# The head of a one-layer encoder block: tile 0 scaled ahead of the first low part, norm_g's row spread by two fp32r products, low parts reordered, roots taken from the sum

## The chip, the cores and the metric

The kernel runs on one core of a Trainium2 chip, as one launch. The metric is the device time of one execution in microseconds, the median over several runs. A profile of one execution gives each engine's instructions with start and duration: PE (matrix products; PEld loads its weights), DVE (VectorE), ACT (ScalarE), POOL (GpSimd) and SP, whose queue issues most transfers.

## What is computed

One layer of a gated hybrid block on x of 1024 x 1024 (float32), then a last norm:

```python
def rmsnorm(x, g):
    y = x * lax.rsqrt(jnp.mean(x * x, axis=-1, keepdims=True) + EPS)
    return y * g

h = rmsnorm(x, norm_g)
q, k, v, za, u, vs, zs, gm = jnp.split(h @ w_in, IN_SPLITS, axis=-1)
a = window_sink_attention(rope(q), rope(k), v, sinks)
a = (a * silu(za)) @ w_att_out
sgo = chunked_spatial_gating(gelu(u), gelu(vs), sg_w, sg_b, sg_ln_g, sg_ln_b)
sgo = (sgo * silu(zs)) @ w_sg_out
ga, gs = jnp.split(sigmoid(gm + b_merge), 2, axis=-1)
x = x + (ga * a + gs * sgo) @ w_o
out = rmsnorm(x, final_g)
```

The change concerns three things in it: the first norm of h, the first products of h (with the columns of `vs`), and the reciprocal roots of all norms.

## The kernel before

Products in float32 are made of three products in fp32r, a float32 format that PE reads in one go: each operand is split into a high part (a cast on ACT, `hi`) and a low part (the operand minus its high part, mostly on DVE, `lo`), and high x high, high x low and low x high are summed. Products go by seven instead of eight block products (Strassen-Winograd), which is where the names `b11`, `b21`, `t1`, `b22` and the sums `s1` to `s4` are from.

**The head** brings h into that form, token tile by token tile (128 tokens, `t` from 0 to 7). For a tile, `scale_of` squares the rows on ACT (L545, the sum over a row comes by a read of ACT's accumulator into `ss`), and `rstd_of` (L130) makes the factor 1/root: DVE makes the mean plus EPS (`ve`, L133), ACT its root (L135), DVE the reciprocal (L137), and three small DVE operations one Newton step (L140, L144, L145). `turned_half` scales half of the row by the factor and norm_g (L553, in place), and PE turns it in four 128 x 128 transposes (L557) into a PSUM bank `sc`, of which there are two. `form_of` makes the high part from there on ACT (L568) and the low part on DVE (L569). Tiles 0 to 3 give `b11` and `b21`; tiles 4 to 7 go through `second_tile`, where DVE also subtracts (L595), and ACT copies (L596, L600).

Norm_g is needed on all 128 partitions. Its row lies in one partition (`g_row`); for tiles 0 and 1 PE spreads it by a product of a row of ones with it in float32 (L505) into the two banks `tp` (`g_in`); for the later tiles a transfer brings it (`g_sb`). Products of ones without a use (`keep_busy`, L498) run on PE beside that.

The **first weights** (columns of `vs`) come in four loads, a11 and a12 in two halves each; `split_vs` splits them into high and low parts (L655, L656 for the first half, in two pieces, the second low part on POOL; L155, L156 for the others). `first_product(t)` then makes 24 products of tile t, 12 with a11 into a bank `mm` (or `tp`), 12 with a12 into a bank `o` (all L669), and ACT copies the second away (L687). Later `by_s1` and `by_s4` make the products of tiles 4 to 7 with the sums (L669, ACT's copy L695). Products of the later stages are at L342.

**Order.** Each engine works through its instructions in a fixed order. A scheduler sets that order from the order in which the code issues operations, their dependencies and its own costs; `after(second, first)` binds two instructions of one engine without a wait. Transfers issued on SP run in the order of issue. So code that is written in another order in the head can move instructions of all head tiles on all engines, up to the point where tile 7 is done.

**The tail.** The last product's rows are added to x, squared in two halves on ACT (L1752), the second half's sum goes through `rstd_of` with the first half's mean as `base`, and the row is scaled and stored (L1769 to L1776).

Of the kernel before, what the change touches and what calls it, by code (L numbers as in the profile page):

```python
# [30 lines left out]
P = 128  # L31
# [21 lines left out]
def hybrid_tile(  # L53
# [75 lines left out]

    def rstd_of(ss, scale, base=EPS, n=1):  # L130

        ve = mtile([P, n], F32, f"st{n}", 16 if n == 1 else 5)
        nc.vector.tensor_scalar(ve[:], ss, scale, base, op0=ALU.mult, op1=ALU.add)  # L133
        rt = mtile([P, n], F32, f"st{n}", 16 if n == 1 else 5)
        nc.scalar.activation(rt[:], ve[:], AF.Sqrt)  # L135
# [11 lines left out]

    def split(hi, lo, src, minus=False):
# [5 lines left out]
        else:  # L154
            nc.scalar.copy(hi, src)  # L155
# [339 lines left out]

    def keep_busy(n):
        for _ in range(n):
            nc.tensor.matmul(idle[:], ones_r[:, 0:P], ones_r[:], start=True, stop=True)  # L498

    idle = bank("sc")  # L500
    keep_busy(2)

    g_in = [bank("tp") for half in range(2)]
    for half in range(2):
        nc.tensor.matmul(g_in[half][:], plain[0:1, 0:P], g_row[:, half_of(half)], start=True, stop=True)  # L505
    keep_busy(2)
# [22 lines left out]
    casts, lows, turns = [], [], []  # L529
# [12 lines left out]
    def scale_of(t):  # L542
# [3 lines left out]
        if t == 1 or t > 2:  # L546

            after(square, casts[-1] if t == 1 else casts[2 * t - 3])
        return xt, rstd_of(ss[:], 1.0 / D)

    def turned_half(xt, r, j):
        cs = half_of(j)
        nc.vector.scalar_tensor_tensor(xt[:, cs], xt[:, cs], r[:], g_of[j], op0=ALU.mult, op1=ALU.mult)  # L553
        pt = bank("sc")
        for i in range(4):
            k = j * 4 + i
            turns.append(nc.tensor.transpose(pt[:, i * P : (i + 1) * P], xt[:, k * P : (k + 1) * P], ident[:]))  # L557
        return pt
# [83 lines left out]
    def split_vs(c):  # L642
# [6 lines left out]
        if c:  # L649
            split(hi[:], lo[:], flat(raw))  # L650
        else:

            for k in range(2):
                ks = half_of(k)
                nc.scalar.copy(hi[:, ks], raw[:, k, :])  # L655
                (nc.gpsimd if k else nc.vector).tensor_tensor(  # L656
                    lo[:, ks], raw[:, k, :], hi[:, ks].bitcast(F32), op=ALU.subtract
# [3 lines left out]
    def vs_product(acc, name, t, weight, fresh, last=True, cs=(0, 1)):  # L661
        bh, bl = hb[name]
        for c in cs:
            for n in range(3):
                for k in (2 * c, 2 * c + 1):
# [8 lines left out]
                        stop=k == 3 and n == 2,  # L674
# [7 lines left out]
    def first_product(t):  # L682
        accs[t] = bank("mm" if t < 2 else "tp")
        vs_product(accs[t], "b11", t, "a11", True)
        m2 = bank("o")
        vs_product(m2, "b21", t, "a12", True)
# [38 lines left out]
    for c in (2, 3):  # L725
        split_vs(c)
    for move in unsplit:
# [1184 lines left out]
```

## Time and profile before

| | |
|---|---|
| median of 3 runs | 911.89 us (910.78 to 914.15) |
| the profiled execution | 912.14 us |
| its span, first to last instruction | 910.4 us |
| POOL busy in the span | 141.9 us |
| HBM over the span | 147.74 MB read, 86.11 MB written |

A timeline row reads: start in us, duration, engine, line, operation, output<-input, shapes, count, and in brackets the idle time before it and what ended that. Rows with a count are several instructions; their duration is from the first's start to the last's end. Ends of products on PE are modelled, so two that follow each other overlap in the rows.

### The profile page before, as it was taken

What the parts mean: (1) busy time and instruction counts of PE and PEld (TensorE: products, weight loads), DVE (VectorE), ACT (ScalarE), POOL (GpSimd) and SP (SyncE); (2) the same over time, 40 slices, a digit from 0 to 9 for tenths busy, and PEclk for the clock granted to TensorE, in tenths of its full rate; (3) what the DMA queues carried; (4) which work ended last, traced back from release to release, by engine and by line L of the source; (5) the groups of instructions that cost most, each with busy time, mean ns of one, the idle gap of its engine ahead of it and who ended that gap; (6) DMA issues with size and microseconds to landing.
All of it is one profiled execution on the core that took longest, in us unless ns stands there. A gap on an engine that the chain in (4) does not pass through costs nothing.

```text
span 910.4 us, 13184 instructions
## 1 busy us (share of the span) xinstructions
PE 894.2 (98%) x4284; PEld 743.6 (82%) x4284; DVE 696.8 (77%) x1263; ACT 527.0 (58%) x1059; POOL 141.9 (16%) x204
## 2 busy tenths in 40 slices
PE   8999999999999999999999999999998999999996
PEld 6778888888878788888888888888877887888885
DVE  6869966666676788888878788657797489579986
ACT  7866533334545467767667677654674375367443
POOL 1322222203030001111111011201001111110012
PEclk9999999999999999999999999999999999999999
DMA  9997888858778767788786789899859665998632
GB/s 329 211 250 214 263 204 175 173 153 270 252 235 290 206 181 216 208 178 202 170 239 215 244 224 244 212 345 347 295 192 368 220 197 156 312 307 274 204 120 112
DMA packets 131598, 209.57 MB, mean 230 GB/s; under 512 B 12649, under 2 KB 61033, under 8 KB 131530
## 3 DMA queue, kind: packets, MB, share of 16 engines
q1 hardware_dynamic: 110072, 149.74, 49.7%
q0 software_dynamic: 21312, 58.73, 28.4%
q8 instruction: 34, 0.56, 0.3%
q14 instruction: 34, 0.28, 0.1%
q10 hardware_dynamic: 146, 0.27, 0.1%
HBM read 147.74 MB, written 86.11 MB: 257 GB/s over the span
## 4 chain that ended last, share of the span: by engine, by line
PE 87%; DVE 7%; DMA 2%; issue 1%; ACT 1%; SPq 0%; POOL 0%; DVEq 0%; ACTq 0%
PE ps_mm L342 36%; PE ps_o L342 26%; PE ps_sc L1242 3%; PE ps_tp L342 3%; PE ps_mm L669 3%; PE ps_tp L669 2%; PE ps_o L1327 2%; PE ps_sc L342 2%; PE ps_tp L1286 2%; PE ps_o L669 2%; PE ps_tp L917 2%; PE ps_sc L669 1%; DVE wl L156 1%; DVE bq L185 1%; DMA q_hl<-qhl 1%
## 5 line engine op out<-in xcount | busy, mean ns | idle before, releaser
L155 ACT CAST wh<-s 128x1024 fp32r<-128x1024 f32 (+1 forms) x79 | 79.2, 1005 | 96.0 <-PE ps_mm L342 52.0
L156 DVE TENSOR_TENSOR wl<-wr,wh 128x512 fp32r<-128x512 f32 (+1 forms) x77 | 72.0, 936 | 51.8 <-ACT wh L155 51.0
L156 DVE TENSOR_TENSOR wl<-s,wh 128x1024 fp32r<-128x1024 f32 (+1 forms) x79 | 92.5, 1171 | 12.3 <-ACT wh L155 12.1
L155 ACT CAST wh<-wr 128x512 fp32r<-128x512 f32 (+1 forms) x77 | 63.0, 820 | 58.4 <-PE ps_mm L342 30.4
L342 PE MATMUL ps_o<-T_t1h,wh 128*128 128x512 f32 x148 | 58.8, 397 | 0.8 <-ACT wh L155 0.7
L342 PE MATMUL ps_o<-T_b22h,wh 128*128 128x512 f32 x148 | 58.3, 394 | 0.0
L342 PE MATMUL ps_mm<-T_b11h,wl 128*128 128x512 f32 x140 | 55.4, 396 | 2.9 <-DVE wl L156 2.9
L342 PE MATMUL ps_o<-T_b22l,wh 128*128 128x512 f32 x148 | 57.9, 391 | 0.0
L342 PE MATMUL ps_o<-T_b22h,wl 128*128 128x512 f32 x148 | 57.7, 390 | 0.0
L342 PE MATMUL ps_o<-T_t1h,wl 128*128 128x512 f32 x148 | 57.7, 390 | 0.0
L342 PE MATMUL ps_o<-T_t1l,wh 128*128 128x512 f32 x148 | 57.6, 389 | 0.0
L1255 ACT ACTIVATE pr<-ps_sc,sm 128x192 f32<-128x192 f32 (+2 forms) x128 | 50.9, 410 | 9.0 <-DVE sm L1251 6.6
L342 PE MATMUL ps_mm<-T_b11h,wh 128*128 128x512 f32 x140 | 55.3, 395 | 0.0
L342 PE MATMUL ps_mm<-T_t4h,wh 128*128 128x512 f32 x140 | 55.3, 395 | 0.0
L342 PE MATMUL ps_mm<-T_t2h,wh 128*128 128x512 f32 x140 | 54.7, 391 | 0.6 <-ACT x L360 0.6
L342 PE MATMUL ps_mm<-T_t3l,wh 128*128 128x512 f32 x140 | 54.6, 390 | 0.6 <-DVE T_t3l L156 0.6
L342 PE MATMUL ps_mm<-T_b11l,wh 128*128 128x512 f32 x140 | 55.2, 394 | 0.0
L342 PE MATMUL ps_mm<-T_t3h,wh 128*128 128x512 f32 x140 | 54.9, 392 | 0.0
L342 PE MATMUL ps_mm<-T_t4h,wl 128*128 128x512 f32 x140 | 54.7, 391 | 0.0
L342 PE MATMUL ps_mm<-T_t3h,wl 128*128 128x512 f32 x140 | 54.7, 390 | 0.0
L342 PE MATMUL ps_mm<-T_t2h,wl 128*128 128x512 f32 x140 | 54.6, 390 | 0.0
L342 PE MATMUL ps_mm<-T_t2l,wh 128*128 128x512 f32 x140 | 54.6, 390 | 0.0
(389 smaller groups left out, 2395.2 us busy)
## 6 DMA issues: line engine op xcount, KB each, us to landing
wr<-in_w_dram SPq DMA_DIRECT2D x86, 256.0 KB
sums<-in_w_dram POOLq DMA_DIRECT2D x20, 512.0 KB, 6.7
s<-sums SPq DMA_DIRECT2D x20, 512.0 KB
q_hl<-qhl SPq DMA_DIRECT2D x16, 512.0 KB
q<-q_hl SPq DMA_DIRECT2D x64, 128.0 KB
y_dr<-x POOLq DMA_DIRECT2D x28, 256.0 KB, 6.5
g<-in_w_dram POOLq DMA_DIRECT2D x12, 512.0 KB, 6.0
wr<-in_w_dram SPq DMA_DIRECT2D x11, 512.0 KB
```

Source lines behind the costliest of these rows:

```text
L155: nc.scalar.copy(hi, src)
L156: return nc.vector.tensor_sub(lo, src, hi.bitcast(F32))
L185: op(dst[:, i : i + 2, :], a[:, i : i + 2, :], c[:, i : i + 2, :])
L342: nc.tensor.matmul(acc, lt, rt, start=fresh and k == 0 and n == 0, stop=k == 3 and n == 2, skip_group_check=True,)
L669: mm = nc.tensor.matmul(acc[:], lt, rt, start=fresh and k == 0 and n == 0, stop=k == 3 and n == 2, skip_group_check=True,)
L917: nc.tensor.matmul(pm[:, t * P : (t + 1) * P], xh[:, half * 4 + t, g * P : (g + 1) * P], bias[-1][1][:, g % 4, :], start=True, stop=True,)
L1242: nc.tensor.matmul(sc[:, i, k0:], q_of[:, c, i * P : (i + 1) * P], kt[:, f, k0:], start=f == 0, stop=f == 1,)
L1255: nc.scalar.activation(held_in[c, i], sc[:, i, lo:hi], AF.Exp, bias=nmax[:, c, i : i + 1], scale=-1.0, accum_out=sums[:, c, i : i + 1],)
L1286: nc.tensor.transpose(dst, pr[:, i, block * P : block * P + width], ident[:])
L1327: nc.tensor.matmul(po[:, cs], lt, rt, start=n == 0, stop=n == len(terms) - 1)
```

## The change

Roots are taken from the sum itself (ACT's activation does scale and bias, `of_root`), with the mean made beside it on DVE. Norm_g's row is split into two fp32r parts and spread by four products among eleven from a first string of ten `keep_busy` products, whose order `feed` binds. The second token tile's load is issued before the second weight half, its square stands ahead of tile 0's first cast, and tile 0's scaling stands ahead of the first weight low part. Tile 0's products take their terms in another order.

```diff
     def rstd_of(ss, scale, base=EPS, n=1):
         ve = mtile([P, n], F32, f"st{n}", 16 if n == 1 else 5)
-        nc.vector.tensor_scalar(ve[:], ss, scale, base, op0=ALU.mult, op1=ALU.add)
+        of_mean.append(nc.vector.tensor_scalar(ve[:], ss, scale, base, op0=ALU.mult, op1=ALU.add))
         rt = mtile([P, n], F32, f"st{n}", 16 if n == 1 else 5)
-        nc.scalar.activation(rt[:], ve[:], AF.Sqrt)
+        of_root.append(nc.scalar.activation(rt[:], ss, AF.Sqrt, bias=eps_sb[:] if base is EPS else base, scale=scale))
...
+    def feed(mm):
+        if fed:
+            after(mm, fed[-1])
+        fed.append(mm)
+
     def keep_busy(n):
         for _ in range(n):
-            nc.tensor.matmul(idle[:], ones_r[:, 0:P], ones_r[:], start=True, stop=True)
+            feed(nc.tensor.matmul(idle[:], ones_r[:, 0:P], ones_r[:], start=True, stop=True))
 
     idle = bank("sc")
-    keep_busy(2)
-
     g_in = [bank("tp") for half in range(2)]
+    g_both = slot("t1h")
+    g_parts = [g_both[0:1, 2 * n : 2 * n + 2, :] for n in range(2)]
     for half in range(2):
-        nc.tensor.matmul(g_in[half][:], plain[0:1, 0:P], g_row[:, half_of(half)], start=True, stop=True)
-    keep_busy(2)
+        hi, lo = (part[:, half, :] for part in g_parts)
+        src = g_row[:, half_of(half)]
+        nc.scalar.copy(hi, src)
+        (nc.gpsimd if half else nc.vector).tensor_tensor(lo, src, hi.bitcast(F32), op=ALU.subtract)
+
+    def spread(n, half):
+        part = g_parts[n][:, half, :]
+        feed(
+            nc.tensor.matmul(g_in[half][:], ones_r[0:1, 0:P], part, start=n == 0, stop=n == 1, skip_group_check=True)
+        )
+
+    keep_busy(6)
+    spread(0, 0)
+    spread(0, 1)
+    spread(1, 0)
+    keep_busy(1)
+    spread(1, 1)
+    keep_busy(3)
...
-        if t == 1 or t > 2:
-
-            after(square, casts[-1] if t == 1 else casts[2 * t - 3])
+        squares.append(square)
+        if t > 2:
+
+            after(square, casts[2 * t - 3])
...
         if c:
-            split(hi[:], lo[:], flat(raw))
+            first_lows.append(split(hi[:], lo[:], flat(raw)))
         else:
 
             for k in range(2):
                 ks = half_of(k)
-                nc.scalar.copy(hi[:, ks], raw[:, k, :])
+                after(nc.scalar.copy(hi[:, ks], raw[:, k, :]), of_root[0])
...
-    def vs_product(acc, name, t, weight, fresh, last=True, cs=(0, 1)):
+    def vs_product(acc, name, t, weight, fresh, last=True, cs=(0, 1), terms=(0, 1, 2)):
...
     def first_product(t):
         accs[t] = bank("mm" if t < 2 else "tp")
-        vs_product(accs[t], "b11", t, "a11", True)
+        terms = (0, 1, 2) if t else (0, 2, 1)
+        vs_product(accs[t], "b11", t, "a11", True, terms=terms)
...
-    unsplit = first_tile(0)
+    first = scale_of(0)
     for name, at in (("a11", "t3h"), ("a12", "t3l")):
         raws[name] = slot(at, dt=F32)
     load_vs(0)
+    x_in[1] = load_x(1)
     load_vs(1)
+    first_lows = []
     split_vs(0)
-    x_in[1] = load_x(1)
+    second = scale_of(1)
+    unsplit = first_tile(0, first)
+    after(of_mean[1], lows[0])
+    after(first_lows[0], scalings[1])
+    after(lows[0], first_lows[0])
     split_vs(1)
-    second = scale_of(1)
+    after(first_lows[2], lows[0])
+    after(lows[1], first_lows[2])
+    after(casts[0], squares[1])
+    after(hi_of[0], casts[0])
+    after(casts[1], hi_of[0])
...
     for c in (2, 3):
         split_vs(c)
+        after(first_lows[c + 1], lows[1])
+        after(hi_of[c - 1], casts[1])
...
     first_tile(1, second)
+    after(scalings[2], first_lows[4])
...
-    nc.vector.tensor_scalar(ones[:], ident[:], 0.0, 1.0, op0=ALU.mult, op1=ALU.add)
+    after(nc.vector.tensor_scalar(ones[:], ident[:], 0.0, 1.0, op0=ALU.mult, op1=ALU.add), lows[-1])
```

How this moves the built program's rows, at three places. Line numbers of the changed program are some 20 to 50 higher: L553 is there L582, L569 L601, L568 L600, L545 L572, L656 L689, L156 L160, L155 L159, L695 L730, L596 L628, L557 L587, L669 L703.

DVE in the head, from tile 0's reciprocal to tile 0's second low part (`wr_119` is tile 0 of x, `wl` are weight low parts, `st` the small statistics), before:

```order
L137 RECIPROCAL st_23_147<-st_22_145 128x1
L140 SCALAR_TENSOR_TENSOR st_24_149<-st_21_143,st_23_147 128x1
L144 TENSOR_SCALAR st_24_149<-st_24_149 128x1
L145 TENSOR_TENSOR st_24_149<-st_24_149,st_23_147 128x1
L656 TENSOR_TENSOR wl_174<-T_t3h_169,wh_173 128x512
L553 SCALAR_TENSOR_TENSOR wr_119<-wr_119,st_24_149,ps_tp_126 128x512
L553 SCALAR_TENSOR_TENSOR wr_119<-wr_119,st_24_149,ps_tp_127 128x512
L156 TENSOR_TENSOR wl_182<-T_t3h_169,wh_181 128x1024
L569 TENSOR_TENSOR T_b11l_133<-ps_sc_154,T_b11h_132 128x4x128
L569 TENSOR_TENSOR T_b21l_135<-ps_sc_162,T_b21h_134 128x4x128
L813 TENSOR_SCALAR ones_719<-ident 128x128
```

and now:

```order
L147 TENSOR_TENSOR st_25_162<-st_25_162,st_24_160 128x1
L582 SCALAR_TENSOR_TENSOR wr_119<-wr_119,st_25_162,ps_tp_124 128x512
L582 SCALAR_TENSOR_TENSOR wr_119<-wr_119,st_25_162,ps_tp_125 128x512
L689 TENSOR_TENSOR wl_173<-T_t3h_166,wh_172 128x512
L601 TENSOR_TENSOR T_b11l_146<-ps_sc_191,T_b11h_145 128x4x128
L135 TENSOR_SCALAR st_32_180<-st_31_178 128x1
L160 TENSOR_TENSOR wl_207<-T_t3h_166,wh_206 128x1024
L139 RECIPROCAL st_34_184<-st_33_182 128x1
L601 TENSOR_TENSOR T_b21l_148<-ps_sc_199,T_b21h_147 128x4x128
```

Both scalings stand ahead of the first weight low part, each weight low part has changed places with a token low part, and `ones` is gone from here.

ACT in the head and again at tiles 6 and 7 (`wT` is where the squares go, `ps_sc` a turned half), in the head before:

```order
L135 ACTIVATE st_22_145<-st_21_143 128x1
L655 CAST wh_173<-T_t3h_169 128x512 x2
L155 CAST wh_181<-T_t3h_169 128x1024
L568 CAST T_b11h_132<-ps_sc_154 128x4x128
L568 CAST T_b21h_134<-ps_sc_162 128x4x128
L545 ACTIVATE wT_136,st_34_185<-wr_179 128x1024
L155 CAST wh_214<-T_t3l_170 128x1024
```

and now:

```order
L137 ACTIVATE st_23_158<-st_21_154,eps_sb 128x1
L687 CAST wh_172<-T_t3h_166 128x512 x2
L572 ACTIVATE wT_149,st_31_178<-wr_169 128x1024
L600 CAST T_b11h_145<-ps_sc_191 128x4x128
L159 CAST wh_206<-T_t3h_166 128x1024
L137 ACTIVATE st_33_182<-st_31_178,eps_sb 128x1
L600 CAST T_b21h_147<-ps_sc_199 128x4x128
L159 CAST wh_227<-T_t3l_167 128x1024
```

Tile 1's square (`wr_169`, before `wr_179`) has moved ahead of tile 0's first cast, and the second weight cast behind it. At tiles 6 and 7 ACT had, from tile 7's square on:

```order
L545 ACTIVATE wT_136,st_110_577<-wr_212 128x1024
L695 ACTIVATE xh_116<-ps_o_563 128x512
L596 ACTIVATE x_139<-ps_sc_544 128x512
L568 CAST T_t1h_380<-xh_116 128x4x128
L600 COPY T_t4l_384<-ps_sc_554 128x512
L135 ACTIVATE st_112_581<-st_111_579 128x1
```

and now has:

```order
L572 ACTIVATE wT_149,st_111_590<-wr_225 128x1024
L628 ACTIVATE x_152<-ps_sc_557 128x512
L600 CAST T_t1h_393<-xh_116 128x4x128
L632 COPY T_t4l_397<-ps_sc_567 128x512
L730 ACTIVATE xh_116<-ps_o_576 128x512
L137 ACTIVATE st_113_594<-st_111_590,eps_sb 128x1
```

The copy of a finished product (`ps_o`) has moved behind tile 6's three operations.

PE at tile 4 (`ps_o_418` is tile 2's second product, `ps_tp_464` tile 3's first, `T_t1l` holds tile 4 of x), before:

```order
L669 MATMUL ps_o_418<-wh_214,T_b21l_135 128x512 x2
L669 MATMUL ps_o_418<-s_218,T_b21h_134 128x512 x2
L669 MATMUL ps_o_418<-s_219,T_b21h_134 128x512 x2
L669 MATMUL ps_o_418<-s_218,T_b21l_135 128x512 x2
L557 MATMUL ps_sc_386<-ident,T_t1l_205 128x128 x4
```

and now:

```order
L703 MATMUL ps_o_431<-wh_227,T_b21l_148 128x512 x2
L587 MATMUL ps_sc_399<-ident,T_t1l_218 128x128 x4
L703 MATMUL ps_o_431<-s_231,T_b21h_147 128x512 x2
L703 MATMUL ps_o_431<-s_232,T_b21h_147 128x512 x2
L703 MATMUL ps_o_431<-s_231,T_b21l_148 128x512 x2
```

Tile 4's first transposes stand six products sooner; tile 3's first likewise, those of tiles 5 to 7 by up to three products.

More of the change, by code (lines that the diff above doesn't have):

```diff
@@ L154, in split @@
         else:
-            nc.scalar.copy(hi, src)
+            hi_of.append(nc.scalar.copy(hi, src))
             return nc.vector.tensor_sub(lo, src, hi.bitcast(F32))
@@ L528, in hybrid_tile @@
     g_of = list(g_in)
-    casts, lows, turns = [], [], []
+    casts, lows, turns, scalings, squares = [], [], [], [], []
     def add_on(dst, src):
@@ L673, in vs_product @@
                         start=fresh and k == 0 and n == 0,
-                        stop=k == 3 and n == 2,
+                        stop=k == 3 and n == terms[-1],
                         skip_group_check=True,
```

19 lines of the change are left out of this document (14 added, 5 removed).

## The prediction

> **What bounds the kernel now.** I read the page first, then the waits of PE, the chain of waits over the first 53 us, and the timelines of single engines. The page says that PE decides nearly everywhere:
>
> ```profile
> PE 894.2 (98%) x4284; PEld 743.6 (82%) x4284; DVE 696.8 (77%) x1263; ACT 527.0 (58%) x1059; POOL 141.9 (16%) x204
> PE 87%; DVE 7%; DMA 2%; issue 1%; ACT 1%; SPq 0%; POOL 0%; DVEq 0%; ACTq 0%
> ```
>
> The first is busy time, the second the chain that ended last. What the edits touch lies in the first 53 us and in the last 10, so the windows there say how much idle PE has to give up (columns: PE busy, PEld, DVE, ACT, POOL, granted clock, DMA share, GB/s):
>
> ```profile
> 8.90:12.30 3.40, 3.40 (x12) 2.74 (x11) 2.73 (x5) 2.82 (x6) 0.00 (x0) 1.00 1.01 411
> 12.30:18.20 5.90, 5.75 (x29) 4.24 (x27) 4.40 (x10) 4.73 (x11) 1.93 (x2) 1.00 0.96 378
> 18.20:45.60 27.40, 27.29 (x137) 21.90 (x138) 24.09 (x54) 22.49 (x44) 6.83 (x8) 1.00 0.99 223
> 45.60:52.70 7.10, 6.50 (x33) 4.86 (x31) 5.12 (x12) 3.32 (x8) 3.50 (x4) 1.00 1.01 290
> ```
>
> From 18.2 to 45.6 PE idles 0.11 us, and from 45.6 to 52.7 it idles 0.60. So a start of tile 1's products that is earlier by some amount is carried by a full PE to 45.6; there the chain leaves PE and runs over ACT and DVE through tile 7 until PE goes on at 52.69. DMA is at its limit in all these windows, so loads do not come sooner than now. Nothing in the head can give much: these are tenths of 910 us.
>
> **The change part by part.** First tile 0, whose chain is in the timelines of DVE and ACT:
>
> ```profile
> 5.46 0.19 ACT L545 ACTIVATION_READ_ACCUMULATOR wT<-wr 128x1 f32 x1
> 5.68 0.15 DVE L133 TENSOR_SCALAR st<-st 128x1 f32<-128x1 f32 x1 [3.82 <-ACT wT L545]
> 5.87 0.20 ACT L135 ACTIVATE st<-st 128x1 f32<-128x1 f32 x1 [0.22 <-DVE st L133]
> 6.74 0.16 DVE L145 TENSOR_TENSOR st<-st,st 128x1 f32<-128x1 f32 x1
> 6.83 0.69 DVE L656 TENSOR_TENSOR wl<-T_t3h,wh 128x512 fp32r<-128x512 f32 x1
> 7.44 1.40 DVE L553 SCALAR_TENSOR_TENSOR wr<-wr,st,ps_tp 128x512 f32<-128x512 f32 x2
> 8.05 1.05 ACT L155 CAST wh<-T_t3h 128x1024 fp32r<-128x1024 f32 x1 [0.95 <-DMA T_t3h<-in_w_dram]
> 9.41 0.59 ACT L568 CAST T_b11h<-ps_sc 128x512 fp32r<-128x512 f32 x1 [0.31 <-PE ps_sc L557]
> ```
>
> The root waits no longer for DVE's mean: it starts at 5.69 where it started at 5.87, so DVE's last factor comes at 6.56, not 6.74. With the low part (L656) moved behind the scaling, the first half is scaled 0.19 us after that (the step from 15.67 to 15.86 below), at 6.75 instead of 7.44: 0.69 us sooner. Is norm_g's row there by then? PE's rows at the start:
>
> ```profile
> 1.92 2.07 PE L498 MATMUL ps_sc<-T_b22l 128*128 128x512 f32 x4 [1.92 <-DVE T_b22l L494]
> 3.92 3.78 PE L505 MATMUL ps_tp<-wh,wl 1*128 1x512 f32 x4
> 8.28 1.94 PE L557 MATMUL ps_sc<-ident,wr 128*128 128x128 f32 x8 [0.58 <-issue]
> 11.06 1.05 PE L669 MATMUL ps_mm<-wl,T_b11h 128*128 128x512 f32 x2
> 11.92 0.82 PE L669 MATMUL ps_mm<-wh,T_b11l 128*128 128x512 f32 x2
> ```
>
> Two products start every 0.86 us (11.06 to 11.92), 0.43 each. The two old products with norm_g held PE for 3.78 us. The new string has 14 products of 512 columns in fp32r: PE is free at 1.92 + 14 x 0.43 = 7.94, or 8.1 with the slower first. The seventh to ninth and the eleventh are norm_g's; the eleventh ends near 6.9, the second half is scaled at 7.42. So neither half waits. Their inputs cost two casts of one row on ACT, one low part on DVE, one on POOL. A one-row operation is not in the trace; the nearest are 0.5 us on ACT, 0.69 on DVE (L656) and 1.47 on POOL, all for 128 rows of the same length. I take these, since the length along the row is the same; at nothing, or at double, they still fit: ACT and DVE have nothing else until the square at 4.50, and POOL would be ready at 5.3, with double at 6.8 against PE's need at 6.2, which costs at most 0.6 of a string that has 0.3 to spare.
>
> So the transposes can start near 8.1 (8.28 before) and the first high part 1.13 later (8.28 to 9.41), at 9.2. But ACT now does tile 1's square ahead of it, and that square waits for tile 1's load, now third in SP's queue. The third load was seen at 8.05 (the row of ACT L155, which waited for it). A square holds ACT for 1.05 us:
>
> ```profile
> 10.74 1.06 ACT L545 ACTIVATE wT<-wr 128x1024 f32<-128x1024 f32 x1
> 11.79 1.03 ACT L155 CAST wh<-T_t3l 128x1024 fp32r<-128x1024 f32 x1
> 9.31 0.33 SPq L722 DMA_DIRECT2D T_t1l<-in_x_dram  x1
> ```
>
> That gives 9.10. Both ways meet: **9.15 instead of 9.41**, so of the 0.69 us only 0.26 arrive. The weight half that was third is now fourth, seen by 9.31 (SP's issue that waits for the fourth); its cast comes at 9.66 behind the high part, so 0.35 us of cover; without the cover it costs what it is late.
>
> From there DVE sets the pace to tile 1:
>
> ```profile
> 12.86 1.23 DVE L156 TENSOR_TENSOR wl<-T_t3l,wh 128x1024 fp32r<-128x1024 f32 x1 [0.78 <-ACT wh L155]
> 15.67 0.15 DVE L145 TENSOR_TENSOR st<-st,st 128x1 f32<-128x1 f32 x1
> 15.86 1.40 DVE L553 SCALAR_TENSOR_TENSOR wr<-wr,st,ps_tp 128x512 f32<-128x512 f32 x2
> 16.86 1.18 PE L557 MATMUL ps_sc<-ident,wr 128*128 128x128 f32 x8
> 17.54 0.59 ACT L568 CAST T_b11h<-ps_sc 128x512 fp32r<-128x512 f32 x1
> ```
>
> In the new order: high part 9.15 to 9.74, low part 9.77; ACT's weight cast 9.66 to 10.71, DVE's weight low part 10.74, the second token low part 11.95, the next weight's 12.8, the last 14.0 (a 1,024-wide one takes 1.23, the next starts 1.14 after it), the factor at 15.15, tile 1 scaled at 15.34: 0.52 sooner. PE, which had run into it from behind (transposes at 16.86 although the half was scaled at 16.6), now stands ready, so the transposes start at about 16.2 and tile 1's first high part at 16.9 instead of 17.54. **First term: -0.6 us**; its bounds are 0 (the waits for loads eat it) and -0.7. Reordering the terms of tile 0's products costs nothing: the same 24, with the low part that is ready first asked for first.
>
> Second, tile 7: rows of PE, ACT and DVE along the chain of waits from 45 on, with PE's two waits in brackets:
>
> ```profile
> 45.39 0.62 PE L669 MATMUL ps_o<-wh,T_b22h 128*128 128x512 f32 x2
> 45.59 0.60 ACT L695 ACTIVATE xh<-ps_o 128x512 f32<-128x512 f32 x1 [0.45 <-PE ps_o L669]
> 46.09 0.59 ACT L596 ACTIVATE x<-ps_sc 128x512 f32<-128x512 f32 x1
> 49.18 1.41 DVE L553 SCALAR_TENSOR_TENSOR wr<-wr,st,xh 128x512 f32<-128x512 f32 x2
> 50.22 0.63 PE L557 MATMUL ps_sc<-ident,wr 128*128 128x128 f32 x4 [0.36 <-DVE wr L553]
> 52.69 0.50 PE L669 MATMUL ps_sc<-T_t2h,T_t1h 128*128 128x512 f32 x1 [0.24 <-ACT x L596]
> ```
>
> ACT copied a product (L695) for which it had to wait 0.45 us, with tile 6's work (L596 and the high part) queued behind it and tile 7's root behind that. In the changed program this copy stands behind tile 6's three operations. Tile 7's scaling thereby comes some 0.5 us sooner on top of the first term, which takes PE's 0.36 and most of the 0.24. **Second term: -0.6 us**, all of the idle in the window; bounds 0 and -0.9 (the latter if from 45.39 PE's 24 products at 0.23, the 0.62 of a pair less the 0.39 of one, and two stretches of transposes at 0.45 simply followed one another: 51.8 for 52.69).
>
> Third, the tail, where every hop counts once because nothing is left to hide it:
>
> ```profile
> 904.38 0.21 DVE L133 TENSOR_SCALAR st<-st,st 128x1 f32<-128x1 f32 x1 [0.20 <-ACT ps_tp L1752]
> 904.63 0.20 ACT L135 ACTIVATE st<-st 128x1 f32<-128x1 f32 x1 [0.28 <-DVE st L133]
> ```
>
> The last root starts 904.63 - 904.38 = 0.25 us sooner, since its mean is made beside it. **Third term: -0.25**, with bounds 0 and -0.3. The middle root, of eight means at once, lies beside a full PE and counts nothing. The constant `ones`, 0.2 us of DVE moved from 11.5 to after 60, is already in the DVE chain above.
>
> Sum: -0.6 - 0.6 - 0.25 = **-1.45 us**. The profiled execution took 912.14 with a span of 910.4; the rest, 1.74, lies outside the span and stays. It goes to 910.7. The median shown, 911.89, is 0.25 below that execution, so I say **910.5**.
>
> PE's pace deserves a look. Products start 0.43 us apart until 12.3 and 0.23 apart later, while the clock column reads 1.00 throughout; the same happens once more:
>
> ```profile
> 688.48 0.79 PE L342 MATMUL ps_mm<-T_b11h,wl 128*128 128x512 f32 x1 [1.75 <-DVE wl L156]
> 691.86 0.39 PE L342 MATMUL ps_mm<-T_t4h,wl 128*128 128x512 f32 x1
> ```
>
> After an idle 1.75 us some eight products go at 0.43 ((691.86 - 688.48) / 0.43). The Trainium skill ("TensorE: Matmul & The Clock Gate", section "What's actually happening") says that a gate halves PE's clock until a free-running window of about 3.4 us has been busy. By that rule the fuller string of products would open the gate sooner, or, with the window out of step, no sooner than now; the trace agrees with the pace, and cannot show the phase. In my sum the pace does not matter as long as it changes by 12.3, because PE waits for ACT at 9.15 and for DVE at 15.3 either way.
>
> **The rivals.** *Tile 7's wait comes back* (0.20): L695 moves only the place where ACT waits, and PE idles as before. Then -0.6 - 0.25: 911.0. For it speaks that DVE is busy 24.09 of 27.4 us before that point; against it that the 0.45 was spent with the needed work queued behind.
>
> *The hoisted transposes stall PE* (0.13), the case on the other side. PE's program now asks for the transposes of tile 3 six products sooner and for those of tile 4 six sooner, 6 x 0.23 = 1.4 us each:
>
> ```profile
> 24.45 1.42 DVE L553 SCALAR_TENSOR_TENSOR T_t1l<-T_t1l,st,xh 128x512 f32<-128x512 f32 x2
> 26.10 0.60 PE L557 MATMUL ps_sc<-ident,T_t1l 128*128 128x128 f32 x4
> ```
>
> If DVE gets ahead by the first term alone, tile 3's first half is ready at 24.45 + 0.85 - 0.6 = 24.7, and PE asks for it at 26.10 - 1.4 - 0.6 = 24.1: 0.6 us of stall; at tile 4 up to the whole 1.4, and some 0.3 at tiles 5 and 6. It decides once the stalls exceed the 1.45 gained; at 2.3 the result is +0.9: 912.8. Against it: DVE's new order makes tile 3's factor before tile 2's low parts (it was behind them), which brings that scaling about 0.6 us sooner again.
>
> *A late change of pace* (0.04): if the 0.43 lasts to 15.7, 14 of tile 0's 24 products are done by then and tile 1 starts 1.1 late instead of 0.6 early: about 912.7.
>
> *The change doesn't do what it says* (0.07): the scaling is sooner but the wait for tile 1's load swallows all of it; only the tail counts: 911.6.
>
> *More* (0.06): the string's timing also spares the slow stretch at 688, eight times 0.2 us: 908.9.
>
> **How the numbers follow.** The forecast has 0.50. Executions of the same kernel lie between 910.78 and 914.15, so the range is not set by the cases alone: 908.4 to 912.9 holds the forecast with about 2 us either way, the wait that comes back, the hidden case and most of the stalls. About 0.5% (4.6 us) is what a measurement of this kernel can tell from no change; no case reaches it, and only scatter or something unseen would: faster 0.05, within 0.92, slower 0.03.
>
> **What would show it.** Right: tile 0's scaling near 6.75, its first high part near 9.15 straight behind tile 1's square, tile 1's near 16.9, PE's idle before 52 gone, the last root straight behind the last square. Wrong: a PE wait of over half a microsecond at the transposes of tiles 3 to 6, tile 1's load seen after 8.5, or products 0.43 apart beyond 13.

## The result and the profile after

| | median us | from | to | runs |
|---|---|---|---|---|
| before | 911.48 | 909.72 | 914.15 | 22 |
| changed | 909.59 | 907.79 | 911.55 | 22 |

The ratio is 0.9979 with a 95% interval from 0.9971 to 0.9987: the change takes off 1.2 to 2.6 us, well inside what was called no change (4.6 us), and the median lies 0.9 below the 910.5 predicted. The profiled execution took 911.38 with a span of 909.6, against 912.14 and 910.4 before. So the two profiles differ by only 0.8, and the rows must be read with the scatter between executions in mind.

The page's busy times and its chain by engine read as before; PE still sets nearly everything:

```profile
PE 895.0 (98%) x4290; PEld 745.0 (82%) x4290; DVE 698.1 (77%) x1264; ACT 530.0 (58%) x1061; POOL 143.3 (16%) x205
PE 87%; DVE 8%; DMA 2%; issue 2%; ACT 1%; SPq 0%; DVEq 0%; ACTq 0%
```

**Tile 0.** The timelines of PE, DVE and ACT at the start of the changed kernel (start, duration, engine, line; in brackets the idle time ahead):

```profile
1.91 2.93 PE L509 MATMUL ps_sc<-T_b22l 128*128 128x512 f32 x6 [1.91 <-DVE T_b22l L498]
4.77 1.64 PE L524 MATMUL ps_tp<-T_t1h,T_b22l 1*128 1x512 f32 x3
6.34 0.80 PE L509 MATMUL ps_sc<-T_b22l 128*128 128x512 f32 x1
7.07 0.79 PE L524 MATMUL ps_tp<-T_t1h,T_b22l 1*128 1x512 f32 x1
7.79 1.65 PE L509 MATMUL ps_sc<-T_b22l 128*128 128x512 f32 x3
9.24 1.91 PE L587 MATMUL ps_sc<-ident,wr 128*128 128x128 f32 x8
...
7.01 1.63 DVE L582 SCALAR_TENSOR_TENSOR wr<-wr,st,ps_tp 128x512 f32<-128x512 f32 x2
...
7.85 1.06 ACT L572 ACTIVATE wT<-wr 128x1024 f32<-128x1024 f32 x1 [0.62 <-DMA wr<-in_x_dram]
10.33 0.59 ACT L600 CAST T_b11h<-ps_sc 128x512 fp32r<-128x512 f32 x1 [1.33 <-PE ps_sc L587]
```

DVE goes the way that was forecast, though not as far: the scaling starts at 7.01 (7.44 before, 6.75 forecast). But PE ends its string at 9.24, not at 7.94 to 8.1, ACT waits 1.33 us for the transposes, and tile 0's first high part comes at 10.33, 0.92 later than before instead of 0.26 sooner. The starts show where the time is: six products take 2.86 us, three 1.57, one 0.73, one 0.72, three 1.45. At 0.43 each that would be 2.58, 1.29, 0.43, 0.43 and 1.29. The first four stretches are too long by 0.28 to 0.30, and each ends where products of 128 rows (`128*128`) and of one row (`1*128`) change over; the last is too long by 0.16. Product by product, each of the four changes costs 0.29 (0.13 ahead of the first product of the new height, 0.16 behind it), 1.16 together; the first product of the whole string costs 0.16 more, which the prediction had as "the slower first". PE's weight loads (PEld) show where it goes:

```profile
4.77 0.92 PEld L524 LDWEIGHTS ps_tp<-T_t1h,T_b22l 1*128 1x128 f32 x3 [0.65 <-ACT T_t1h L518]
6.34 0.29 PEld L509 LDWEIGHTS ps_sc<-T_b22l 128*128 128x128 f32 x1 [0.65 <-issue]
7.07 0.28 PEld L524 LDWEIGHTS ps_tp<-T_t1h,T_b22l 1*128 1x128 f32 x1 [0.44 <-issue]
7.79 0.50 PEld L509 LDWEIGHTS ps_sc<-T_b22l 128*128 128x128 f32 x2 [0.44 <-issue]
```

At each change the load starts together with its own product and takes 0.28 to 0.29 us, as much as the change costs. Between products of the same height the load starts while the product before is still running (at 4.94 for the product at 5.36).

Tile 1's first high part on ACT is late by the same cause, 18.02 against 16.9 forecast and 17.54 before:

```profile
18.02 0.59 ACT L600 CAST T_b11h<-ps_sc 128x512 fp32r<-128x512 f32 x1 [0.19 <-PE ps_sc L587]
```

**Tile 7.** The window (columns as before), and the rows of ACT, DVE and PE along that chain:

```profile
45.60:52.70 7.10, 7.04 (x35) 5.59 (x35) 5.60 (x13) 3.78 (x9) 3.51 (x4) 1.00 0.97 295
```

```profile
45.48 0.60 ACT L628 ACTIVATE x<-ps_sc 128x512 f32<-128x512 f32 x1 [0.45 <-DVE xh L627]
...
46.97 0.61 ACT L730 ACTIVATE xh<-ps_o 128x512 f32<-128x512 f32 x1
...
48.86 1.41 DVE L582 SCALAR_TENSOR_TENSOR wr<-wr,st,xh 128x512 f32<-128x512 f32 x2
...
49.71 0.63 PE L587 MATMUL ps_sc<-ident,wr 128*128 128x128 f32 x4
```

The first row's 0.45 is a wait for DVE, not for a product. The product's copy (L730, L695 before) now stands behind tile 6's work, the transposes of tile 7 wait for nothing, and PE idles 0.06 us where it idled 0.60.

**The tail.** The mean (DVE) and the root (ACT) of the last row start together:

```profile
903.76 0.29 ACT L137 ACTIVATE st<-st,st 128x1 f32<-128x1 f32 x1
...
903.76 0.21 DVE L135 TENSOR_SCALAR st<-st,st 128x1 f32<-128x1 f32 x1
904.09 0.16 DVE L139 RECIPROCAL st<-st 128x1 f32<-128x1 f32 x1
```

From the start of the last product to the end there are 7.72 us, 7.97 before.

### The profile page after: what moved, and what is told of

Read it like the earlier page. It is cut to its first block, busy times and chain, and to the rows that moved or that the text cites. A ratio compares the mean times of both kernels' runs of the same rounds, so it can differ in the third digit from the quotient of the medians.

```text
span 909.6 us, 13196 instructions
## 1 busy us (share of the span) xinstructions
PE 895.0 (98%) x4290; PEld 745.0 (82%) x4290; DVE 698.1 (77%) x1264; ACT 530.0 (58%) x1061; POOL 143.3 (16%) x205
## 4 chain that ended last, share of the span: by engine, by line
PE 87%; DVE 8%; DMA 2%; issue 2%; ACT 1%; SPq 0%; DVEq 0%; ACTq 0%
PE ps_mm L346 36%; PE ps_o L346 27%; PE ps_sc L1290 3%; PE ps_tp L346 3%; PE ps_mm L703 2%; PE ps_o L703 2%; PE ps_tp L703 2%; PE ps_o L1375 2%; PE ps_tp L1334 2%; PE ps_sc L346 2%; PE ps_tp L965 2%; DVE wl L160 1%; PE ps_sc L703 1%; DVE bq L189 1%; DMA wr<-in_w_dram 1%
## 5 line engine op out<-in xcount | busy, mean ns | idle before, releaser
L159 ACT CAST wh<-s 128x1024 fp32r<-128x1024 f32 (+1 forms) x79 | 79.3, 1006 | 95.6 <-PE ps_mm L346 51.3
L160 DVE TENSOR_TENSOR wl<-wr,wh 128x512 fp32r<-128x512 f32 (+1 forms) x77 | 72.0, 936 | 53.6 <-ACT wh L159 53.0
L160 DVE TENSOR_TENSOR wl<-s,wh 128x1024 fp32r<-128x1024 f32 (+1 forms) x79 | 92.6, 1172 | 12.2 <-ACT wh L159 11.9
L159 ACT CAST wh<-wr 128x512 fp32r<-128x512 f32 (+1 forms) x77 | 63.1, 821 | 59.3 <-PE ps_mm L346 30.7
```

The lines of the kernel that those rows point to most:

```text
L159: hi_of.append(nc.scalar.copy(hi, src))
L160: return nc.vector.tensor_sub(lo, src, hi.bitcast(F32))
```

## The experiments

One measure serves for nearly all: the start of the same PE product (counted back from the last), minus its start in the first profile of the kernel before. The table gives the start of tile 1's first product, and by how much each stretch then grew or shrank against that first profile. "Pace" is where products 0.43 us apart give way to 0.23.

| profile | pace | tile 1 starts | 18-48 | 48-55 | 55-240 | 240-335 | 335-680 | 680-700 | 700-901 |
|---|---|---|---|---|---|---|---|---|---|
| before | 12.3 | 18.18 | 0 | 0 | 0 | 0 | 0 | 0 | 0 |
| before_2 | 13.3 | 18.54 | 0.00 | -0.04 | 0.31 | -0.09 | -0.03 | 0.13 | 0.00 |
| before_3 | 12.7 | 18.15 | -0.03 | 0.05 | 0.36 | -0.94 | 0.02 | 0.15 | 0.01 |
| before_4 | 13.2 | 18.34 | 0.00 | 0.03 | 0.14 | -0.06 | -0.03 | 0.13 | 0.02 |
| changed | 11.4 | 18.65 | 0.00 | -0.82 | 0.17 | -1.15 | 0.13 | -0.03 | 0.69 |
| again | 13.7 | 19.21 | 0.00 | -0.79 | 0.06 | -1.29 | 0.00 | -1.48 | 0.07 |
| tail_mean | 13.7 | 19.24 | 0.02 | -0.79 | 0.03 | -1.54 | -0.09 | -1.45 | 0.80 |
| copy_first | 5.6 | 17.94 | 0.05 | -0.60 | 0.14 | -1.67 | 0.10 | -1.48 | 0.61 |
| copy_lead | 11.7 | 18.66 | 0.00 | -0.10 | 0.09 | -1.53 | 0.13 | -1.48 | 0.65 |
| dense | 10.0 | 17.68 | 0.05 | -0.78 | 0.32 | -1.32 | 0.09 | 1.41 | 0.35 |
| dense_2 | 11.2 | 17.53 | -0.01 | -0.78 | 0.02 | -1.69 | -0.10 | -1.47 | 0.51 |
| dense_low | 15.1 | 19.79 | 0.04 | -0.76 | 0.16 | -1.07 | -0.16 | -1.47 | 0.66 |
| dense_low2 | 13.4 | 18.39 | -0.01 | -0.79 | 0.16 | -1.42 | -0.07 | -1.43 | 0.51 |
| wide | 7.2 | 17.30 | 0.40 | -0.78 | 0.13 | -1.70 | 0.04 | 0.16 | 0.11 |

**The change again** (no edit).

> The changed kernel once more, to see whether the profiled execution was typical. String theory (the 14 products take 7.3 us instead of 6.2, since a product of one row and one of 128 rows can't have their weights loaded beside each other): the same in every execution, so tile 0's first high part is again at 10.3 (within 0.1) and tile 1's at 18.0, and the time is 909.6, 1.9 below the kernel before. Rival (the change of PE's pace falls differently in each execution, and the profiled one was an unlucky one): in this profile the pace changes before 8 us and tile 0's high part comes near 9.2; if it is at 10.3 again with the pace changing after 11, the rival falls.

909.88 us, ratio 0.9981 (0.9972 to 0.9989): the gain is real. The high part of tile 0 came at 10.34, so the string is no accident of one execution. PE's rows show that the pace did differ, later still (0.43 up to 13.7):

```profile
12.85 1.05 PE L703 MATMUL ps_mm<-wl,T_b11h 128*128 128x512 f32 x2
13.71 0.70 PE L703 MATMUL ps_mm<-wh,T_b11h 128*128 128x512 f32 x2
```

Here tile 0's products last so long that tile 1's high part comes at 18.57, not at 18.0 as expected, and its products start at 19.21. By the sign named ahead, the rival falls as the cause of the late high part of tile 0. But the pace adds or takes another half microsecond at tile 1, and the run copy_first below shows that it can shorten the string too.

**The string without alternation.**

```
     spread(1, 0)
-    keep_busy(1)
     spread(1, 1)
-    keep_busy(3)
+    keep_busy(2)
```

> The four products with norm_g's parts follow one another, and the string is 12 products instead of 14: six of ones, the four, two of ones. String theory: only two changes of height are left, 0.28 us each; string from 1.91 to 1.91 + 12 x 0.43 + 2 x 0.28 = 7.6 or 7.8, transposes at 7.9 (behind DVE's first half, 7.01 + 0.85), tile 0's first high part at 9.05 behind tile 1's square instead of 10.33, tile 1 scaled near 15.2 instead of 16.35, its high part near 16.9 instead of 18.02; the time 0.8 to 1.1 us below the change's, about 908.6. Rival (behind tile 0 it is the loads and DVE that set tile 1, or what is gained meets the same late sums before 52 us): tile 0's high part is sooner, tile 1's is not, or the products behind 52 start where they did; 909.6.

```profile
4.77 2.07 PE L524 MATMUL ps_tp<-T_t1h,T_b22l 1*128 1x512 f32 x4
6.78 1.22 PE L509 MATMUL ps_sc<-T_b22l 128*128 128x512 f32 x2
7.83 1.97 PE L586 MATMUL ps_sc<-ident,wr 128*128 128x128 f32 x8
...
8.32 1.06 ACT L571 ACTIVATE wT<-wr 128x1024 f32<-128x1024 f32 x1 [1.11 <-DMA wr<-in_x_dram]
...
9.38 0.56 ACT L599 CAST T_b11h<-ps_sc 128x512 fp32r<-128x512 f32 x1
```

This edit takes out two of the four changes of height and two products, so it doesn't tell the one from the other; the run wide below does. PE is ready at 7.83, and what holds the high part to 9.38 is now tile 1's square, whose load came at 8.3. Tile 1's products start at 17.68, 0.97 sooner than in the changed kernel, and 0.88 of that is still there at 55 us (-0.50 + 0.05 - 0.78 against +0.47 - 0.82). The loads and DVE behind tile 0 were not the limit; that rival falls. The time was 908.27 us, ratio 0.9968 (0.9959 to 0.9978), although its profiled execution, 911.52, was the slowest of the set.

> The dense string again, since its first median (908.27 of 10 runs) stands 1.3 to 1.6 below the change's, about as far as these medians scatter. If the string costs what its profile shows (tile 1's products 0.97 sooner than in the change at the same change of pace), 908.3 to 909.0 again and a ratio of 0.9965 to 0.997; if the first set was luck, 909.6 and 0.998.

907.93 us, ratio 0.9965 (0.9952 to 0.9978), and tile 1 at 17.53 with the pace of the changed kernel (11.2 against 11.4). Twice the fastest version: its medians beat both kernels, though its intervals still touch the change's.

**Products of full height.** The alternation stays; rows 1 to 127 of norm_g's parts are zeros.

```
+    for n in range(4):
+        nc.vector.tensor_scalar(g_both[:, n, :], plain, 0.0, None, op0=ALU.mult)
...
-        part = g_parts[n][:, half, :]
+        part = g_both[:, 2 * n + half, :]
         feed(
-            nc.tensor.matmul(g_in[half][:], ones_r[0:1, 0:P], part, start=n == 0, stop=n == 1, skip_group_check=True)
+            nc.tensor.matmul(g_in[half][:], ones_r[:, 0:P], part, start=n == 0, stop=n == 1, skip_group_check=True)
```

> The string keeps its 14 products and their order, but norm_g's parts are spread by products of 128 rows (rows 1 to 127 are zeros, written by four more operations on DVE between 1.9 and 3.7, where it is idle), with the same weights as the products of ones. String theory: all 14 start 0.43 apart, from 1.91 to 7.94 as the prediction had it; transposes at 8.0, tile 0's first high part 9.1 to 9.2, tile 1's near 16.9; the time as with the dense string, about 908.6. Rival one (what makes them late is the wait for norm_g's parts, not the height): the gaps of 0.55 to 0.72 us between starts stay, tile 0's high part at 10.3, 909.6. Rival two (loads and DVE set tile 1): sooner at tile 0, unchanged behind it, 909.6.

```profile
4.64 1.48 PE L526 MATMUL ps_tp<-T_t1h,T_b22l 128*128 128x512 f32 x3
5.92 0.63 PE L509 MATMUL ps_sc<-T_b22l 128*128 128x512 f32 x1
6.35 0.63 PE L526 MATMUL ps_tp<-T_t1h,T_b22l 128*128 128x512 f32 x1
6.78 1.01 PE L509 MATMUL ps_sc<-T_b22l 128*128 128x512 f32 x3
7.99 1.38 PE L589 MATMUL ps_sc<-ident,wr 128*128 128x128 f32 x8 [0.20 <-DVE wr L584]
...
9.00 0.57 ACT L602 CAST T_b11h<-ps_sc 128x512 fp32r<-128x512 f32 x1
```

Same order and same data, but now one product every 0.43 (4.64 to 5.92 is three, 5.92 to 6.35 one, 6.35 to 6.78 one). So the change of height was the cost, not the wait for norm_g's parts. The high part comes at 9.00 and tile 1 at 17.30, the earliest of all. Of the 0.88 ahead of the old kernel 0.40 is lost again at tile 4 (tile 3's transposes, at 23.96, wait for nothing):

```profile
29.61 0.63 PE L589 MATMUL ps_sc<-ident,T_t1l 128*128 128x128 f32 x4 [0.44 <-DVE T_t1l L584]
```

The hoisted transposes wait for DVE, as the rival had it, once tile 1 is early enough. The time was 909.86 us, ratio 0.9979 (0.9971 to 0.9988): no better than the change, and the forecast of 908.6 missed. In 9 of its 11 runs the mean granted clock was 0.997 or less, in 2 it was 0.998 (908.07 and 908.54 us); how that goes with time stands in the last section.

**The weight's low part ahead of the scaling**, in the dense string.

```
-    after(first_lows[0], scalings[1])
-    after(lows[0], first_lows[0])
+    after(scalings[0], first_lows[0])
```

> The dense string, but with the first low part of the weight ahead of tile 0's scaling on DVE again, as the kernel before had it. Theory (with the string out of the way, scaling first is worth something): the low part takes DVE from about 6.9 to 7.6, tile 0's first half is scaled at 7.65 instead of 7.03, transposes at 8.4 instead of 7.83, tile 0's first high part at 9.55 instead of 9.0 to 9.4, later by 0.15 to 0.55 according to when tile 1's square ends. Rival (tile 1's square sets that high part anyway): transposes later, high part and everything behind it the same within 0.1.

The timeline shows more than was asked for. The last factor (L147, one value per row) fell behind the low part, and there it took 1.23 us instead of 0.16, to the end of POOL's low part:

```profile
7.13 1.29 POOL L688 TENSOR_TENSOR wl<-T_t3h,wh 128x512 fp32r<-128x512 f32 x1 [1.97 <-ACT wh L686]
7.20 1.23 DVE L147 TENSOR_TENSOR st<-st,st 128x1 f32<-128x1 f32 x1
...
8.52 1.41 DVE L581 SCALAR_TENSOR_TENSOR wr<-wr,st,ps_tp 128x512 f32<-128x512 f32 x2
```

So this run did not test the order alone. The next one adds `after(first_lows[0], ...)` on that last factor:

> The dense string with the weight's first low part ahead of tile 0's scaling, now behind the last factor of tile 0's root, exactly where the kernel before had it (in the run before, the factor stood behind the low part and DVE was held there by POOL's low part for 1.23 us). Theory: the low part takes DVE from 7.0 to 7.6, the scaling starts at 7.6 instead of 7.03 to 7.11, the transposes at 8.4 instead of 7.83 to 7.91, tile 0's first high part at 9.5 instead of 9.23 to 9.38. Rival (POOL's low part holds DVE in any order): scaling again at 8.4 to 8.5, high part after 10.2.

```profile
6.71 0.69 DVE L688 TENSOR_TENSOR wl<-T_t3h,wh 128x512 fp32r<-128x512 f32 x1
...
7.32 1.40 DVE L581 SCALAR_TENSOR_TENSOR wr<-wr,st,ps_tp 128x512 f32<-128x512 f32 x2
...
9.27 0.59 ACT L599 CAST T_b11h<-ps_sc 128x512 fp32r<-128x512 f32 x1
```

The load came early in this execution (square of tile 0 at 4.48). Against that square the scaling starts 2.84 later, in both dense runs 2.40 (7.03 behind 4.63, 7.11 behind 4.71). So the order is worth 0.44 us at the scaling, and at the high part (4.79 behind the square, 4.75 and 4.52) 0.04 to 0.27: tile 1's square hides the rest. Tile 1 itself starts at 18.39 here, mostly since the pace changed at 13.4.

**ACT's copy put back.** First ahead of tile 6's first copy only:

```
         copied = nc.scalar.mul(x_place(1, 1, t), t5s[t][:], -1.0)
+        if t == 1:
+            after(negated[2], copied)
```

> ACT again copies the finished product (L730 here, L695 before) ahead of tile 6's own copy, as the kernel before did; all else as in the change. Theory (the copy's place was worth what the second term says): ACT waits some 0.45 us for that product with tile 6's work behind it, PE idles 0.3 to 0.6 us more between 45 and 53 us, and the products behind 53 us start 0.5 to 0.85 later than in the change; time 910.1 to 910.5. Rival (in the changed kernel tile 7's gain comes from the scaling order, not from the copy): PE idles no more than 0.1 us there and the time is 909.6.

909.61 us, ratio 0.9983 (0.9971 to 0.9995), with 0.60 still gained between 48 and 55: tile 6's high part had slipped ahead of the copy. Neither theory was tested; then with both bound (`after(casts[-2], copied)` besides):

> The last run bound the finished product's copy ahead of tile 6's first copy only, and the high part of tile 6's sum slipped ahead of it. Here the copy stands ahead of both, ACT's order at tile 6 of the kernel before. The measure is how much the products gain on the kernel before between 48 and 55 us, which was 0.78 to 0.82 us in four profiles with the change's order and 0.60 with the last run's. Theory (the copy's place carries the second term): no more than 0.2 us is gained there, and PE idles 0.4 to 0.6 us between 45.6 and 52.7. Rival (something else of the change carries it): 0.6 us or more is gained again.

```profile
46.07 0.60 ACT L731 ACTIVATE xh<-ps_o 128x512 f32<-128x512 f32 x1 [1.02 <-PE ps_o L703]
...
53.05 0.50 PE L703 MATMUL ps_sc<-T_t2h,T_t1h 128*128 128x512 f32 x1 [0.25 <-ACT x L628]
```

ACT waits 1.02 us for the product again, and only 0.10 is gained instead of 0.79 to 0.82. PE's idle time was smaller than expected in the window named (0.12), with 0.25 more just behind it. The place of one copy, with the transposes that the scheduler moves along with it, carries 0.7 of the 0.8.

The first of the two runs had another use. Its string is the change's, and its pace changed at 5.6:

```profile
4.77 1.22 PE L524 MATMUL ps_tp<-T_t1h,T_b22l 1*128 1x512 f32 x3
5.92 0.50 PE L509 MATMUL ps_sc<-T_b22l 128*128 128x512 f32 x1
...
7.97 1.38 PE L587 MATMUL ps_sc<-ident,wr 128*128 128x128 f32 x8 [0.23 <-DVE wr L582]
```

At the fast pace even the alternating string is done before the scaling. The same string gives a start of tile 1 at 17.94 or at 19.24, according to when the pace changes.

**The last roots from the mean.**

```
-        of_root.append(nc.scalar.activation(rt[:], ss, AF.Sqrt, bias=eps_sb[:] if base is EPS else base, scale=scale))
+        if base is EPS:
+            of_root.append(nc.scalar.activation(rt[:], ss, AF.Sqrt, bias=eps_sb[:], scale=scale))
+        else:
+            of_root.append(nc.scalar.activation(rt[:], ve[:], AF.Sqrt))
```

> The change, but the roots of the output rows are again taken from DVE's mean (the roots of the head and the middle stay as changed). Theory: from the start of the last product to the end 7.97 us as in the kernel before instead of 7.72 to 7.73, and nothing moves ahead of it. Rival (these roots also set when PE gets its last weights near 837 us, where the changed kernel loses 0.05 to 0.66 us on the kernel before): that loss is gone too.

7.98 us from the last product to the end, and 0.80 lost between 700 and 901. The tail is the root's; the loss there is not.

**The kernel before, three times more** (no edit).

> The kernel before once more, for what differs between its executions. If PE's pace changes at another time than 12.3 us, it shows what the old head does with it: with a change before 8 us I expect tile 0's high part still at 9.4 (it hangs on DVE) and tile 1's products still at 18.0 to 18.2 (they hang on DVE too); with one after 13 us, later by the products still at 0.43. If the two waits of PE at 272 and 315 us (1.1 us together) are the old kernel's own, they are there again; if they belong to that execution, they are not. The tail from the last product's start to the end is 7.97 us again.

> The kernel before a third time. Between 240 and 335 us its first two profiles lost 0.98 and 1.3 us of PE to waits (272 and 315 us; 315 us), the kernels with the change 0 to 0.3. If such waits are the old kernel's own, PE waits about 1 us there again; if they come with the execution, 0 to 0.3. Tile 7's wait does not hang on the execution: PE idles 0.3 to 0.6 us between 45.6 and 52.7 again. PE's pace changes at any time from 5 to 15 us.

> The kernel before a fourth time, for the same question: about 1 us of waits between 240 and 335 us if they are the old kernel's own, 0 to 0.3 if they come with the execution; and, with the third, where tile 1's products start for two more times of the change of pace (so far 18.18 with the change at 12.3 us and 18.54 at 13.0).

The waits of PE between 55 and 335 us, in that order:

```profile
PE ps_sc L1242 <- ACT pr L1255: 1.3, 1, 1.3
```

```profile
PE ps_sc L1242 <- ACT pr L1255: 0.4, 1, 0.4
```

```profile
PE ps_mm L342 <- DVE x L377: 0.7, 1, 0.7
PE ps_sc L1242 <- ACT pr L1255: 0.4, 1, 0.4
```

The wait at 272 us belonged to the first execution (the last has one of its own, 0.7 at 303 us); that for ACT's `pr` was in all four profiles of the old kernel (0.4, 1.3, 0.4, 0.4) and in two of ten with the change, with 0.3. Tile 7's wait was there every time (the stretch 48-55 agrees within 0.05), and so was the tail of 7.98. Tile 1 started between 18.15 and 18.54.

Of copy_lead, dense_low, dense_low2, tail_mean and these three there is one execution each: 910.13, 910.91, 909.06 and 910.19 us, and 912.79, 911.74 and 912.53. Single times can't tell differences of a microsecond, so these runs are read by their rows alone.

## Why the prediction came out

The total was right and its parts were not. Means over the profiles of each kernel (before: four; change: five with its string, three with its string and its copy, ten for the stretches that all share):

| part | predicted | measured |
|---|---|---|
| head, to tile 1 | -0.6 | 18.74 - 18.30 = +0.44 |
| tile 7 | -0.6 | -0.80 - 0.01 = -0.81 |
| 55 to 335 us | 0 | -1.31 - (-0.07) = -1.24 |
| 700 to 901 us | 0 | 0.50 - 0.01 = +0.49 |
| tail | -0.25 | -0.25 |
| sum | -1.45 | -1.37 |

The stretches left out come to less than 0.02 on the mean (without the 0.40 of wide), but for 680-700, which hangs on the execution (last section). Two errors cancelled, which is luck: a head that lost, and a middle that gained. The measured change of the medians, -1.9 (-2.6 to -1.2), agrees with either sum.

*The first term failed*, at "PE is free at 1.92 + 14 x 0.43 = 7.94, or 8.1 with the slower first". The count, the 0.43 and the slower first were right: in the full-height run the products start 0.43 apart up to the twelfth at 6.78 (the last two already go at the faster pace). But four changes of height cost 0.29 us each, 1.16 in all: 8.1 became 9.24. The trace of before had one such change: four products of ones take 2.00 us ahead of the first of L505 (1.92 to 3.92), where 4 x 0.43 and the slower first make 1.88, and the first product of L505 takes 0.16 longer than its others (starts 1.02, 0.85 and 0.85 apart). It was there to be read and was not priced. The term measured +0.44, outside its bounds of 0 to -0.7, which held the late loads as the only danger. The step "of the 0.69 us only 0.26 arrive" was right in kind: with the dense string the high part came at 9.23 and 9.38 behind tile 1's square.

*The root* of tile 0 gained 0.10, not 0.18: from the start of the sum's read to the last factor it is 1.18 us (5.58 to 6.76) instead of 1.28 (5.46 to 6.74), since the root with a scale and a bias takes 0.30 us and the plain one 0.20.

*Pace.* "The pace does not matter as long as it changes by 12.3" was wrong in its condition: in two of five profiles it changed at 13.7, and tile 1 started 0.56 to 0.59 later than with 11.4. That is a milder form of the rival called the late change of pace (to 15.7, with a chance of 0.04 and 1.7 us of price); it is common, and costs a third of that. It also matters ahead of 12.3: at 5.6 the string itself is shorter.

*The second term* held, -0.81 for -0.6 and inside its bounds, and by the cause named: with the copy back in its place, and the transposes that move with it, 0.10 is left.

*The third* has its number to the hundredth, and in part by luck. The last root does start 0.25 us sooner (0.22 behind the start of the sum's read, 0.47 before), but it lasts 0.29 instead of 0.20, so 0.15 of it arrive at the reciprocal (0.55 behind the read, 0.70 before). The other 0.09 came ahead of the read, which starts 1.68 us behind the last product's start (1.77 before): the root of the rows before is sooner as well, and with it the scaling on ACT that stands ahead of the last square.

*The stall of the hoisted transposes* did not come in the change, whose head is late. It came in the one run where tile 1 was earliest, and at another tile than expected: nothing at tile 3, where 0.6 was estimated, 0.44 at tile 4 (up to 1.4), and nothing at tiles 5 and 6.

*Unforeseen* are the two middle stretches. Between 60 and 855 us the engines' orders are the same in both kernels, so the times of transfers and buffers must differ. Ahead of the loss near 837 us ACT waits longer for a transfer that goes out to memory and back (`bq`, near 833 us): 1.16 to 1.46 us in the four profiles of the old kernel, 1.65 to 2.38 in the ten with the change; in the changed kernel's first profile, with 2.23, PE then waits 0.32 for DVE's low part. The two shortest of the ten, 1.65 and 1.67, go with the smallest losses (0.11 and 0.07).

Why ACT's `pr` is in time at 315 us in eight of ten profiles with the change and in none of the old kernel stays open, as does the loss near 837. Neither hangs on the place of the copy, on the string, on the last roots or on the scaling ahead of the first low part, since the runs without them (copy_lead, dense, tail_mean, dense_low2) show both. What is left of the change (the roots in the head and the middle, the order of the loads and of the other low parts and casts, the order of terms) was not tried alone.

## What to carry to other kernels

Before you fill PE with spare products, check that neighbours have the same height: here products of one row among products of 128 rows cost 0.29 us at each change, and filling them up with zero rows took that cost away. In an engine's fixed order look for a copy that waits, with needed work queued behind it: moving one such copy was worth 0.7 us here, and the rebuilt head lost 0.4. Where terms of half a microsecond are at stake, profile the kernel several times before you cost them; four profiles of the old kernel differ by 0.9 us in one stretch.

## What the runs showed of the hardware

**Pace.** The change from 0.43 to 0.23 us came at 12.3 to 13.3 us in the old kernel, at 5.6, 11.4, 11.7 and twice at 13.7 in five runs of one and the same string with one-row products, and at 7.2 with rows of full height. The Trainium skill ("TensorE: Matmul & The Clock Gate", section "What's actually happening") has a free-running window of about 3.4 us that must have been busy; with PE full from 1.9 on, an estimate by it gives a change between 5.3 and 8.7. The full-height string agrees, and so does 5.6. The other four of that string, and the old kernel, are later than the estimate allows, which would fit if a window with many one-row products did not count as busy. A window with some of them does: at 5.6 the products of one row had been running since 4.77. What share decides was not tested.

The same pace decides most of the scatter. After PE's wait of 1.74 us near 687, seven products ran at 0.43 in the changed kernel's profile, and none in the repeat (the first product behind the wait, and two windows around it, columns as before):

```profile
687.28 0.79 PE L346 MATMUL ps_mm<-T_b11h,wl 128*128 128x512 f32 x1 [1.74 <-DVE wl L160]
683.55:686.97 3.42, 1.27 (x5) 0.41 (x3) 3.42 (x4) 1.82 (x3) 0.00 (x0) 1.00 1.04 394
686.97:690.38 3.41, 3.10 (x7) 2.48 (x8) 3.41 (x7) 0.00 (x0) 1.00 (x2) 0.50 1.02 386
```

```profile
687.49 0.50 PE L346 MATMUL ps_mm<-T_b11h,wl 128*128 128x512 f32 x1 [1.74 <-DVE wl L160]
682.86:686.27 3.41, 2.17 (x9) 1.16 (x7) 3.41 (x5) 2.72 (x4) 0.00 (x0) 1.00 1.04 396
686.27:689.69 3.42, 2.20 (x10) 1.83 (x11) 3.42 (x6) 0.00 (x0) 0.54 (x1) 1.00 1.04 385
```

The granted clock (third column from the end) is 0.50 for those 3.41 us. So the prediction's "the clock column reads 1.00 throughout" holds for its windows in the head, where the column reads 1.00 even while products are 0.43 apart, and not here: over 688 to 692 us of its own profile it reads 0.57.

The windows above are no free choice. In all fourteen profiles the time from the change of pace in the head, as the clock's record has it, to the fall of the clock behind the last product is 261, 262 or 263 times 3.413 us, and the slow stretch lies on the same grid. The wait of 1.74 us comes about 0.7 us behind one of 0.7, and what differs between executions is how the grid cuts the two. In the seven profiles with the slow stretch PE was busy for 0.96 to 1.64 us of the window ahead of it; in the other seven no window there had less than 1.73. Half a window is 1.71. This sorts all fourteen, but no run moved the wait or the grid on purpose.

The slow stretch makes steps of 1.4 us in the column 680-700 (the profile of dense, with its 911.52 us, has two such windows in a row). The seven profiles without the slow products have a mean granted clock of 0.998, the seven with them 0.995 to 0.997. The clock so sorts the runs: at 0.998 the medians are 910.9 before (14 runs) and 909.1 and 909.5 with the change (11 and 5), below that 912.3 before (18) and 910.7 and 910.4 with the change (11 and 6). The gain, 1.4 to 1.9 us, is there in both groups.

**DVE beside POOL.** In the run dense_low a DVE operation of 0.16 us on values in SBUF took 1.23 us, until POOL's subtraction ended. The two scalings, which read PSUM as well, were not held so: in the run dense they took 1.40 us beside the same subtraction (7.03 to 8.43, POOL from 7.29 to 8.57). The 1.63 in the changed kernel has another cause: the second scaling starts at 7.90, when the product that brings its half of norm_g, at 7.07, has ended at 7.86. The Trainium skill ("Trainium Architecture — The Big Picture", section "What this means for kernel authors") calls the port that the two engines share an exclusive lock. The run agrees for the one operation that was held; the order of DVE's small operations around a POOL operation can therefore cost more than their length.
